# Eight samples of a head as one wide recurrence, and block sums moved to VectorE, in a one-core decoder layer

## Chip, cores, metric

One NeuronCore of a Trainium2 chip. The metric is the time of one execution on the device in microseconds, the median of several runs. "PE" is TensorE, "DVE" VectorE, "ACT" ScalarE, "POOL" GpSimd, "SP" SyncE, whose queue issues every transfer here.

## What is computed

One inference step of one layer with 512 prompt tokens and 8 single-token samples, 520 columns in all, width 2048, in float32. The part that the first half of the change touches is a gated recurrence of eight heads with a 128 x 128 state:

```python
f = lb + (1 - lb) * sigmoid(z_f);  k = 1 - f
S_t = diag(f_t) S_{t-1} + k_t (outer) i_t
o_t = S_t^T q_t                      # q after silu
```

The prompt starts from a zero state and is done by chunks of 128 tokens with matmuls. Each sample has a state of its own, is one token long, and gives an updated state (an output) and one vector o. The other parts: a gated unit with a layer norm, an output projection, and a dense feed-forward unit `(silu(h @ w_gate) * (h @ w_up)) @ w_down`.

## The kernel before, in words

Every matrix is held transposed, features on the 128 partitions and the 520 tokens along the columns, in two halves of 260. A float32 product is three matmuls of split operands (lines 103 to 105): a weight piece of 128 x 1024 is loaded into one of three raw buffers (`raw_piece`, line 70), ScalarE rounds it to its high part (line 82), VectorE subtracts for the low part (line 84). `pieces` keeps two pieces prepared ahead of the matmuls.

Python generators in the list `behind` are woven into the projections: each call of `step` advances every generator in it by one `yield`. The program order gives priorities; the scheduler of the framework then places an instruction in its engine's queue when its inputs are ready, earlier than in the program where it can. An engine's queue is run in order.

**The heads.** `head(h, w)` (line 321) is such a generator. Its steps, counted by its yields: 1 gates and logs; 2 cumulative sums and the decayed key kh, whose exponential is line 356 and whose last product is line 357; 3 silu of q and level 32; 4 the transpose of kh on PE (line 437) and level 8; 5 nothing; 6 and 7 scores of levels 32 and 8; 8 transpose of the input rows, and of the samples' packed decay, key and query, which go as 24 rows to a scratch tensor in DRAM (`scr`, line 465); 9 and 10 scores of levels 2 and 1; 11 the decays between chunks (matmuls of line 505, VectorE's line 509); 12 the output matmuls (lines 518 and 520); 13 squares; then the norm. Each head brings eight calls of `step`, two for each of its projections z, q, ib and g, so two heads overlap: step 9 of one is followed by step 1 of the next, its step 10 stands beside step 2 of the next, 11 beside 3, 12 beside 4.

**The samples.** The inner generator `samples` (line 469) does a head's eight samples in four pieces of two. A piece loads `bc` (line 475), in which the 24 rows are broadcast to all partitions (decay, key and query of two samples, 3 x 256 columns; one buffer), and two states `S` (line 477). Then VectorE multiplies the states by the decays (line 479), adds key times input, one instruction for each sample (line 483), the states are stored, and VectorE multiplies by the queries (line 486) and sums along the key (line 487). Piece 1 is loaded in step 8 and computed in step 9, where piece 2 is loaded, and so on to step 12.

**Feed-forward.** The first four blocks of columns are products as above. `combine` (line 656) runs beside half of them, and forms the differences of blocks of the activations for a scheme with seven instead of eight block products; of four differences for each of eight k, VectorE makes two (lines 660, 663) and GpSimd two (662, 665), and VectorE splits them (line 113). In the block stage after it, `quarters` (line 700) forms sums of weight blocks for each set of seven products: VectorE lines 717 and 719, GpSimd lines 720 and 725; the sums are split on lines 82 and 84 (their tile is named ws). The products are lines 736 to 738, in `term`.

Of the kernel before, what the change touches and what calls it, by code (L numbers as in the profile page):

```python
# [7 lines left out]
F32 = mybir.dt.float32  # L8
# [4 lines left out]
ALU = mybir.AluOpType  # L13
PSUM = bass.MemoryType.PSUM

P = 128
NP = 512
NS = 8
# [14 lines left out]
def trunk(ctx: ExitStack, tc: tile.TileContext, a: dict):  # L33
    nc = tc.nc
    vec, act, pe, sp = nc.vector, nc.scalar, nc.tensor, nc.sync
# [15 lines left out]
    def bank():  # L51
        return ax.tile([P, 512], F32, tag="ax", name="ax")

    def cols(h):
        return slice(h * HT, (h + 1) * HT)
# [5 lines left out]
    def full(pool, tag, bufs=1, dt=F32):  # L61
        return pool.tile([P, T], dt, tag=tag, name=tag, bufs=bufs)
# [17 lines left out]
    def halved(raw, n=1024):  # L80
        hi = wp.tile([P, 1024], F32R, tag="wh", name="wh", bufs=4)
        act.copy(hi[:, :n], raw[:, :n])  # L82
        lo = wp.tile([P, 1024], F32R, tag="wl", name="wl", bufs=4)
        vec.tensor_tensor(out=lo[:, :n], in0=raw[:, :n], in1=hi[:, :n].bitcast(F32), op=ALU.subtract)  # L84
        return hi, lo
# [22 lines left out]
    def split(x, pool, tag, bufs, scale=None):  # L108
        hi = part(pool, tag, bufs, F32R)
        lo = part(pool, tag, bufs, F32R)  # L110
        if scale is None:
            act.copy(hi, x)
            vec.tensor_tensor(out=lo, in0=x, in1=hi.bitcast(F32), op=ALU.subtract)
        else:
            act.mul(hi, x, scale)
            vec.scalar_tensor_tensor(out=lo, in0=x, scalar=scale, in1=hi.bitcast(F32), op0=ALU.mult, op1=ALU.subtract)
        return hi, lo
# [43 lines left out]
    for i in range(KT):  # L161
# [3 lines left out]
        if i % 4 == 0:  # L165
            c = slice((i % 8) * P, (i % 8 + 4) * P)
# [19 lines left out]
    for k in range(KT):  # L186
        X.append([split(x0[k][:, cols(h)], ap_, "A", 64, g1[:, k:k + 1]) for h in range(2)])
        for m in range(2):
            if k % 8 == 0:
                W[m].append([wp.tile([P, 1024], F32R, tag=t, name=t) for t in ("wh", "wl")])  # L190
            hi, lo = W[m][-1]
            raw = w0[m][k // 8]
            if k % 4 == 0:
                for o, n in ((0, 1), (1, 3)) if k == 0 else ((k % 8, 4),):
                    c = slice(o * P, (o + n) * P)
                    act.copy(hi[:, c], raw[:, c])
                    vec.tensor_tensor(out=lo[:, c], in0=raw[:, c], in1=hi[:, c].bitcast(F32), op=ALU.subtract)
            c = slice((k % 8) * P, (k % 8 + 1) * P)
# [48 lines left out]
    hp = ph1.enter_context(tc.tile_pool(name="hp", bufs=1))  # L247
# [73 lines left out]
    def head(h, w):  # L321
# [3 lines left out]
        k = full(hp, "k")  # L325
# [16 lines left out]
        b = hp.tile([P, NP], F32, tag="b", name="b")  # L342
# [63 lines left out]
        def scores(hh, kk, qq):  # L406
            for c2 in range(2):
                pl = bank()
                for c in range(2):
                    cg = 2 * c2 + c  # L410
                    pe.matmul(pl[:, c * 192:(c + 1) * 192], lhsT=kk[:, cg * P:(cg + 1) * P], rhs=qq[:, cg], start=True, stop=True)  # L411
                pv = pl[:, :384].rearrange("p (c t) -> p c t", c=2)
                Av = A[:, 2 * c2:2 * c2 + 2]
                off = 0
                for j in range(3):
                    n = (3 - j) * hh
                    if hh == 32:
                        act.copy(Av[32 * j:32 * j + 32, :, (j + 1) * 32:], pv[32 * j:32 * j + 32, :, off:off + n])
                        off += n
                    elif hh > 1:  # L420
                        g = 32 // hh
                        for c in range(2):
                            vec.copy_predicated(out=Av[:, c].rearrange("p (g t) -> p g t", g=g)[:, :, (j + 1) * hh:],
                                                mask=masks[hh][:, j * g:(j + 1) * g].unsqueeze(2).to_broadcast([P, g, n]),
                                                data=pv[:, c, off:off + g * n].rearrange("p (g t) -> p g t", t=n))
                        off += g * n
                    elif j < 2:
                        vec.copy_predicated(out=Av[:, j].rearrange("p (g t) -> p g t", t=2)[:, :, 1:2],
                                            mask=mone.unsqueeze(2), data=pv[:, j, 0:64].unsqueeze(2))
                        vec.copy_predicated(out=Av[:, j], mask=mdiag, data=pv[:, j, 64:192])  # L430
# [13 lines left out]
        ib = w["ib"]  # L444
# [19 lines left out]
        scr = tc.dram_tile([24, P], F32, name=f"scr{h}")  # L464
        sp.dma_start(scr, rows)
        ob = full(cc, "C", 16)
        O[8 + h] = ob

        def samples():

            n = 2
            for i in range(0, NS, n):
                bc = hp.tile([P, 3, n * P], F32, tag="bc", name="bc")
                rows_ = scr.rearrange("(a b) k -> a (b k)", a=3)[:, i * P:(i + n) * P]
                sp.dma_start(bc, rows_.partition_broadcast(P))
                S = hp.tile([P, n * P], F32, tag="S", name="S", bufs=2)
                sp.dma_start(S, a["state"][h][:, i * P:(i + n) * P])
                yield
                vec.tensor_tensor(out=S, in0=S, in1=bc[:, 0], op=ALU.mult)
                for b_ in range(n):  # L480
                    c = slice(b_ * P, (b_ + 1) * P)
                    t = NP + i + b_
                    vec.scalar_tensor_tensor(out=S[:, c], in0=bc[:, 1, c], scalar=ib[:, t:t + 1], in1=S[:, c],  # L483
                                             op0=ALU.mult, op1=ALU.add)
                sp.dma_start(a["o_ss"][h][:, i * P:(i + n) * P], S)
                vec.tensor_tensor(out=bc[:, 0], in0=S, in1=bc[:, 2], op=ALU.mult)
                vec.tensor_reduce(out=ob[:, NP + i:NP + i + n].unsqueeze(2), in_=bc[:, 0].rearrange("p (b k) -> p b k", b=n),
                                  op=ALU.add, axis=mybir.AxisListType.X)
            yield

        sg_ = samples()
        next(sg_)
        yield

        scores(2, *lv2)
        next(sg_)
        yield

        scores(1, *lv1)
        next(sg_)  # L500
        yield

        pd = bank()
        for c in range(4):
            pe.matmul(pd[:, c * P:(c + 1) * P], lhsT=kht[:, c], rhs=ibt[:, c], start=True, stop=True)
# [2 lines left out]
        for c in range(1, 4):  # L508
            vec.scalar_tensor_tensor(out=Sc[:, c], in0=Sc[:, c - 1], scalar=dec[:, c], in1=pd[:, c * P:(c + 1) * P],
                                     op0=ALU.mult, op1=ALU.add)  # L510
        sp.dma_start(a["o_sp"][h], Sc[:, 3])
        next(sg_)
        yield

        next(sg_)
        po = bank()
        for c in range(4):
            pe.matmul(po[:, c * P:(c + 1) * P], lhsT=ibt[:, c], rhs=A[:, c], start=True, stop=(c == 0))
            if c:
                pe.matmul(po[:, c * P:(c + 1) * P], lhsT=Sc[:, c - 1], rhs=qh[:, c * P:(c + 1) * P], start=False, stop=True)  # L520
        act.copy(ob[:, :NP], po)
        yield

        sq = full(hp, "e")
# [3 lines left out]
        for i in range(2):  # L528
# [3 lines left out]
                                     op0=ALU.mult, op1=ALU.mult)  # L532
# [123 lines left out]
    def combine():  # L656
        c0, c1 = cols(0), cols(1)
        for k in range(8):
            lo, hi = M[k], M[k + 8]
            vec.tensor_tensor(out=lo[:, c0], in0=lo[:, c1], in1=lo[:, c0], op=ALU.subtract)  # L660
            T1[k] = split(lo[:, c0], tp, "T", 48)
            nc.gpsimd.tensor_tensor(out=lo[:, c1], in0=hi[:, c1], in1=lo[:, c1], op=ALU.subtract)
            vec.tensor_tensor(out=hi[:, c1], in0=hi[:, c1], in1=lo[:, c0], op=ALU.subtract)
            T2[k] = split(hi[:, c1], tp, "T", 48)
            nc.gpsimd.tensor_tensor(out=hi[:, c0], in0=hi[:, c1], in1=hi[:, c0], op=ALU.subtract)
            T3[k] = split(lo[:, c1], tp, "T", 48)
            yield

# [31 lines left out]
    def quarters(w, i, first):  # L700

        raws = {}

        def load(q, src, pool, bufs):
            pool, bufs = (wp, 3) if first else (pool, bufs)
            raws[q] = pool.tile([P, 1024], F32, tag="wr", name="wr", bufs=bufs)
            sp.dma_start(raws[q], src)

        def m1():
            load("11", w[i, 0], wx, 4)  # L710
            load("21", w[i + 1, 0], wx, 4)
            load("22", w[i + 1, 1], wp, 3)
            return halved(raws["11"], 1024)

        def m6():
            s1 = raws["s1"] = wp.tile([P, 1024], F32, tag="wh", name="ws", bufs=4)
            vec.tensor_tensor(out=s1, in0=raws["21"], in1=raws["22"], op=ALU.add)  # L717
            s2 = raws["s2"] = wp.tile([P, 1024], F32, tag="wl", name="ws", bufs=4)
            vec.tensor_tensor(out=s2, in0=s1, in1=raws["11"], op=ALU.subtract)  # L719
            nc.gpsimd.tensor_tensor(out=raws["21"], in0=raws["11"], in1=raws["21"], op=ALU.subtract)  # L720
            load("12", w[i, 1], wp, 3)
            return halved(s2, 1024)

        def m5():
            nc.gpsimd.tensor_tensor(out=raws["s2"], in0=raws["12"], in1=raws["s2"], op=ALU.subtract)
            return halved(raws["s1"], 1024)

        return [m1, m6, m5, lambda: halved(raws["12"], 1024), lambda: halved(raws["21"], 1024),
                lambda: halved(raws["s2"], 1024), lambda: halved(raws["22"], 1024)]
# [13 lines left out]
    c0, c1 = cols(0), cols(1)  # L743
# [214 lines left out]
```

## Time and profile before

| | us |
|---|---|
| median of 3 runs | 2319.09 (2318.36 to 2325.36) |
| the profiled execution | 2318.88 |
| its span, first to last instruction | 2317.2 |
| PE busy | 2266.3 |
| DVE busy | 1664.3 |
| ACT busy | 1065.9 |
| POOL busy | 220.6 |

The span is one execution; a matmul's end is modelled, and busy time of PE is not its peak rate. "PEclk" in a window is the mean granted TensorE clock, 1.00 being 2.4 GHz and 0.50 being 1.2 GHz. The heads run from about 115 to 630 us, the output projection to about 890, the first feed-forward blocks with `combine` to about 975, the block stage to about 1790, the last product after that.

### The profile page before, as it was taken

The numbers are of one execution on the slowest core, as the hardware profiler recorded it, in microseconds if no ns is written. First come the engines' busy times: TensorE is split into PE (matmuls) and PEld (weight loads), VectorE is DVE, ScalarE is ACT, GpSimd is POOL, SyncE is SP. The second block draws the span as 40 slices with busy tenths as digits, with TensorE's granted clock in tenths as the row PEclk, the third lists the DMA queues.
The fourth block names the chain that finished last, engine by engine and source line by source line (L and its number), as shares of the span: only waits on it lengthen the run. The fifth ranks groups of instructions, "written<-read, shape, count | busy, mean of one in ns | idle before, by whom it ended". The sixth has DMA issues, their size and how long they took to land.

```text
span 2317.2 us, 44793 instructions
## 1 busy us (share of the span) xinstructions
PE 2266.3 (98%) x18548; PEld 2256.2 (97%) x18548; DVE 1664.3 (72%) x2688; ACT 1065.9 (46%) x1607; POOL 220.6 (10%) x116
## 2 busy tenths in 40 slices
PE   8999999999999998999999999999999999999998
PEld 8999999999999998999999999999999999999998
DVE  8398777777555778888888888888888534434367
ACT  7286566666345555444343443444334512212155
POOL 0000000000000000322222222222221000000000
PEclk9999999999999999999999999999999999999999
DMA  6224333443335766543333333333333723332275
GB/s 224 92 88 125 113 114 111 120 120 120 115 110 182 214 209 194 176 158 115 115 110 126 119 115 124 119 120 110 118 119 102 229 92 129 112 113 95 90 240 156
DMA packets 130267, 310.16 MB, mean 134 GB/s; under 512 B 14928, under 2 KB 57360, under 8 KB 130064
## 3 DMA queue, kind: packets, MB, share of 16 engines
q1 hardware_dynamic: 130064, 307.30, 42.7%
q8 instruction: 145, 2.38, 0.4%
q14 instruction: 58, 0.48, 0.1%
HBM read 281.64 MB, written 25.61 MB: 133 GB/s over the span
## 4 chain that ended last, share of the span: by engine, by line
PE 80%; DVE 9%; DMA 8%; ACT 1%; issue 1%; SPq 0%; DVEq 0%; POOL 0%; ACTq 0%; POOLq 0%
PE mm L105 14%; PE mm L104 14%; PE mm L103 14%; PE mm L738 8%; PE mm L736 8%; PE mm L737 8%; DMA bc<-scr 5%; PE ax L738 3%; PE ax L736 3%; PE ax L737 3%; DVE wl L84 2%; PE ax L411 1%; DMA scr<-rows 1%; DMA wr<-w_up 1%; DVE S L483 1%
## 5 line engine op out<-in xcount | busy, mean ns | idle before, releaser
L105 PE MATMUL mm<-A,wl 128*128 128x260 f32 x3616 | 1026.2, 284 | 8.7 <-DVE wl L84 8.4
L103 PE MATMUL mm<-A,wh 128*128 128x260 f32 x3616 | 1031.3, 285 | 2.0 <-ACT wh L82 2.0
L104 PE MATMUL mm<-A,wh 128*128 128x260 f32 x3616 | 1026.0, 284 | 0.0
L82 ACT CAST wh<-wr 128x1024 fp32r<-128x1024 f32 (+1 forms) x460 | 475.4, 1035 | 771.6 <-PE mm L104 475.4
L84 DVE TENSOR_TENSOR wl<-wr,wh 128x1024 fp32r<-128x1024 f32 (+1 forms) x460 | 554.7, 1207 | 268.4 <-ACT wh L82 255.8
L105 PEld LDWEIGHTS mm<-A,wl 128*128 128x128 f32 x3616 | 685.0, 189 | 10.5 <-DVE wl L84 10.3
L103 PEld LDWEIGHTS mm<-A,wh 128*128 128x128 f32 x3616 | 684.8, 189 | 2.5 <-ACT wh L82 2.2
L104 PEld LDWEIGHTS mm<-A,wh 128*128 128x128 f32 x3616 | 685.0, 189 | 0.3
L738 PE MATMUL mm<-A,wl 128*128 128x260 f32 x960 | 271.1, 282 | 0.5 <-DVE wl L84 0.5
L737 PE MATMUL mm<-A,wh 128*128 128x260 f32 x960 | 270.8, 282 | 0.0
L736 PE MATMUL mm<-A,wh 128*128 128x260 f32 x960 | 270.4, 282 | 0.0
L82 ACT CAST wh<-ws 128x1024 fp32r<-128x1024 f32 x120 | 123.8, 1047 | 265.8 <-DVE ws L719 265.8
L811 DVE TENSOR_TENSOR Y<-mm,Y 128x260 f32<-128x260 f32 x160 | 68.4, 427 | 193.0 <-PE mm L105 192.8
L84 DVE TENSOR_TENSOR wl<-ws,wh 128x1024 fp32r<-128x1024 f32 x120 | 188.4, 1570 | 11.8 <-ACT wh L82 10.8
L736 PE MATMUL mm<-T,wh 128*128 128x260 f32 x640 | 181.4, 283 | 1.3 <-ACT wh L82 1.3
L738 PE MATMUL mm<-T,wl 128*128 128x260 f32 x640 | 180.8, 282 | 0.8 <-DVE wl L84 0.8
L738 PEld LDWEIGHTS mm<-A,wl 128*128 128x128 f32 x960 | 180.2, 188 | 0.7 <-DVE wl L84 0.7
L737 PEld LDWEIGHTS mm<-A,wh 128*128 128x128 f32 x960 | 180.8, 188 | 0.0
L736 PEld LDWEIGHTS mm<-A,wh 128*128 128x128 f32 x960 | 180.7, 188 | 0.0
L737 PE MATMUL mm<-T,wh 128*128 128x260 f32 x640 | 180.1, 281 | 0.0
L720 POOL TENSOR_TENSOR wr<-wr 128x1024 f32<-128x1024 f32 x40 | 95.8, 2396 | 478.5 <-DVE ws L717 478.5
L719 DVE TENSOR_TENSOR ws<-ws,wr 128x1024 f32<-128x1024 f32 x40 | 134.3, 3358 | 0.0
(229 smaller groups left out, 3123.2 us busy)
## 6 DMA issues: line engine op xcount, KB each, us to landing
wr<-w_gate SPq DMA_DIRECT2D x96, 512.0 KB, 4.0
wr<-w_up SPq DMA_DIRECT2D x96, 512.0 KB, 4.1
wr<-w_down SPq DMA_DIRECT2D x96, 512.0 KB, 3.6
wr<-w_in SPq DMA_DIRECT2D x92, 512.0 KB, 4.1
wr<-w_out SPq DMA_DIRECT2D x64, 512.0 KB, 3.8
bc<-scr SPq DMA_DIRECT2D x32, 384.0 KB, 5.3
G<-fd SPq DMA_DIRECT2D x44, 260.0 KB, 3.9
fd<-G SPq DMA_DIRECT2D x40, 260.0 KB, 3.6
```

Of the source, the lines that this page charges most:

```text
L82: act.copy(hi[:, :n], raw[:, :n])
L84: vec.tensor_tensor(out=lo[:, :n], in0=raw[:, :n], in1=hi[:, :n].bitcast(F32), op=ALU.subtract)
L103: pe.matmul(ps[:, :HT], lhsT=wh[:, c], rhs=xh, start=(k == 0), stop=False)
L104: pe.matmul(ps[:, :HT], lhsT=wh[:, c], rhs=xl, start=False, stop=False)
L105: pe.matmul(ps[:, :HT], lhsT=wl[:, c], rhs=xh, start=False, stop=(k == n - 1))
L411: pe.matmul(pl[:, c * 192:(c + 1) * 192], lhsT=kk[:, cg * P:(cg + 1) * P], rhs=qq[:, cg], start=True, stop=True)
L719: vec.tensor_tensor(out=s2, in0=s1, in1=raws["11"], op=ALU.subtract)
L720: nc.gpsimd.tensor_tensor(out=raws["21"], in0=raws["11"], in1=raws["21"], op=ALU.subtract)
L736: pe.matmul(ps, lhsT=wh[:, c], rhs=xh, start=(start and k == 0), stop=False, skip_group_check=not start)
L737: pe.matmul(ps, lhsT=wh[:, c], rhs=xl, start=False, stop=False, skip_group_check=not start)
L738: pe.matmul(ps, lhsT=wl[:, c], rhs=xh, start=False, stop=(k == len(xs) - 1), skip_group_check=not start)
L811: vec.tensor_tensor(out=Y[m][:, cols(h)], in0=ps, in1=Y[m][:, cols(h)], op=ALU.add)
```

## The change

In `head`, the generator `samples` is gone. Step 8 issues one transfer of all 24 rows to `bc` (now 3 x 1024 columns) and one load of all eight states. Step 10 holds the scores of level 1 and the decays. Step 11 holds two products over 1024 columns, states by decays and keys by inputs; step 12 adds them after the output matmuls, stores the eight states in one transfer, multiplies by the queries and sums. In `combine` and `quarters`, four lines move from GpSimd to VectorE.

```diff
--- before.py
+++ after.py
@@ -466,40 +466,17 @@
         ob = full(cc, "C", 16)
         O[8 + h] = ob
 
-        def samples():
-
-            n = 2
-            for i in range(0, NS, n):
-                bc = hp.tile([P, 3, n * P], F32, tag="bc", name="bc")
-                rows_ = scr.rearrange("(a b) k -> a (b k)", a=3)[:, i * P:(i + n) * P]
-                sp.dma_start(bc, rows_.partition_broadcast(P))
-                S = hp.tile([P, n * P], F32, tag="S", name="S", bufs=2)
-                sp.dma_start(S, a["state"][h][:, i * P:(i + n) * P])
-                yield
-                vec.tensor_tensor(out=S, in0=S, in1=bc[:, 0], op=ALU.mult)
-                for b_ in range(n):
-                    c = slice(b_ * P, (b_ + 1) * P)
-                    t = NP + i + b_
-                    vec.scalar_tensor_tensor(out=S[:, c], in0=bc[:, 1, c], scalar=ib[:, t:t + 1], in1=S[:, c],
-                                             op0=ALU.mult, op1=ALU.add)
-                sp.dma_start(a["o_ss"][h][:, i * P:(i + n) * P], S)
-                vec.tensor_tensor(out=bc[:, 0], in0=S, in1=bc[:, 2], op=ALU.mult)
-                vec.tensor_reduce(out=ob[:, NP + i:NP + i + n].unsqueeze(2), in_=bc[:, 0].rearrange("p (b k) -> p b k", b=n),
-                                  op=ALU.add, axis=mybir.AxisListType.X)
-            yield
-
-        sg_ = samples()
-        next(sg_)
+
+        bc = hp.tile([P, 3, NS, P], F32, tag="bc", name="bc")
+        sp.dma_start(bc.rearrange("p a b k -> p a (b k)"), scr.rearrange("(a b) k -> a (b k)", a=3).partition_broadcast(P))
+        S = hp.tile([P, NS, P], F32, tag="S", name="S")
+        sp.dma_start(S.rearrange("p b k -> p (b k)"), a["state"][h])
         yield
 
         scores(2, *lv2)
-        next(sg_)
         yield
 
         scores(1, *lv1)
-        next(sg_)
-        yield
-
         pd = bank()
         for c in range(4):
             pe.matmul(pd[:, c * P:(c + 1) * P], lhsT=kht[:, c], rhs=ibt[:, c], start=True, stop=True)
@@ -509,16 +486,22 @@
             vec.scalar_tensor_tensor(out=Sc[:, c], in0=Sc[:, c - 1], scalar=dec[:, c], in1=pd[:, c * P:(c + 1) * P],
                                      op0=ALU.mult, op1=ALU.add)
         sp.dma_start(a["o_sp"][h], Sc[:, 3])
-        next(sg_)
-        yield
-
-        next(sg_)
+        yield
+
+        vec.tensor_tensor(out=S, in0=S, in1=bc[:, 0], op=ALU.mult)
+        vec.tensor_tensor(out=bc[:, 1], in0=bc[:, 1], in1=ib[:, NP:].unsqueeze(2).to_broadcast([P, NS, P]), op=ALU.mult)
+        yield
+
         po = bank()
         for c in range(4):
             pe.matmul(po[:, c * P:(c + 1) * P], lhsT=ibt[:, c], rhs=A[:, c], start=True, stop=(c == 0))
             if c:
                 pe.matmul(po[:, c * P:(c + 1) * P], lhsT=Sc[:, c - 1], rhs=qh[:, c * P:(c + 1) * P], start=False, stop=True)
         act.copy(ob[:, :NP], po)
+        vec.tensor_tensor(out=S, in0=S, in1=bc[:, 1], op=ALU.add)
+        sp.dma_start(a["o_ss"][h], S.rearrange("p b k -> p (b k)"))
+        vec.tensor_tensor(out=bc[:, 0], in0=S, in1=bc[:, 2], op=ALU.mult)
+        vec.tensor_reduce(out=ob[:, NP:].unsqueeze(2), in_=bc[:, 0], op=ALU.add, axis=mybir.AxisListType.X)
         yield
 
         sq = full(hp, "e")
@@ -659,10 +642,10 @@
             lo, hi = M[k], M[k + 8]
             vec.tensor_tensor(out=lo[:, c0], in0=lo[:, c1], in1=lo[:, c0], op=ALU.subtract)
             T1[k] = split(lo[:, c0], tp, "T", 48)
-            nc.gpsimd.tensor_tensor(out=lo[:, c1], in0=hi[:, c1], in1=lo[:, c1], op=ALU.subtract)
+            vec.tensor_tensor(out=lo[:, c1], in0=hi[:, c1], in1=lo[:, c1], op=ALU.subtract)
             vec.tensor_tensor(out=hi[:, c1], in0=hi[:, c1], in1=lo[:, c0], op=ALU.subtract)
             T2[k] = split(hi[:, c1], tp, "T", 48)
-            nc.gpsimd.tensor_tensor(out=hi[:, c0], in0=hi[:, c1], in1=hi[:, c0], op=ALU.subtract)
+            vec.tensor_tensor(out=hi[:, c0], in0=hi[:, c1], in1=hi[:, c0], op=ALU.subtract)
             T3[k] = split(lo[:, c1], tp, "T", 48)
             yield
 
@@ -717,12 +700,12 @@
             vec.tensor_tensor(out=s1, in0=raws["21"], in1=raws["22"], op=ALU.add)
             s2 = raws["s2"] = wp.tile([P, 1024], F32, tag="wl", name="ws", bufs=4)
             vec.tensor_tensor(out=s2, in0=s1, in1=raws["11"], op=ALU.subtract)
-            nc.gpsimd.tensor_tensor(out=raws["21"], in0=raws["11"], in1=raws["21"], op=ALU.subtract)
+            vec.tensor_tensor(out=raws["21"], in0=raws["11"], in1=raws["21"], op=ALU.subtract)
             load("12", w[i, 1], wp, 3)
             return halved(s2, 1024)
 
         def m5():
-            nc.gpsimd.tensor_tensor(out=raws["s2"], in0=raws["12"], in1=raws["s2"], op=ALU.subtract)
+            vec.tensor_tensor(out=raws["s2"], in0=raws["12"], in1=raws["s2"], op=ALU.subtract)
             return halved(raws["s1"], 1024)
 
         return [m1, m6, m5, lambda: halved(raws["12"], 1024), lambda: halved(raws["21"], 1024),
```

## Rows read from the trace of the kernel before

**Rows 1.** The page: its first line and part 1, busy time by engine.
```profile
span 2317.2 us, 44793 instructions
...
PE 2266.3 (98%) x18548; PEld 2256.2 (97%) x18548; DVE 1664.3 (72%) x2688; ACT 1065.9 (46%) x1607; POOL 220.6 (10%) x116
```

**Rows 2.** PE's waits: line, releaser: us in total, times, longest.
```profile
PE ax L437 <- DVE kh L357: 15.7, 8, 3.1
...
PE ax L520 <- DVE Sc L509: 5.1, 2, 2.9
...
PE mm L736 <- ACT wh L82: 1.3, 1, 1.3
```

**Rows 3.** Timeline of PE in one head: start, us, engine, line, operation.
```profile
500.67 0.63 PE L437 MATMUL ax<-ident,kh 128*128 128x128 f32 x4 [3.08 <-DVE kh L357]
```

**Rows 4.** Windows: us, busy time of each engine, PEclk, DMA share, GB/s.
```profile
187.00:196.00 9.00, 6.65 (x44) 6.46 (x43) 7.24 (x17) 5.27 (x9) 0.52 (x1) 0.81 0.38 91
...
314.00:326.00 12.00, 8.63 (x49) 8.18 (x48) 10.01 (x28) 4.84 (x8) 0.53 (x1) 0.72 0.42 148
...
437.00:447.00 10.00, 7.35 (x52) 7.19 (x51) 8.90 (x21) 5.50 (x8) 0.53 (x1) 0.83 0.44 141
```

**Rows 5.** VectorE's waits, the line of the samples' first instruction.
```profile
DVE S L479 <- DMA bc<-scr: 57.6, 26, 5.4
```

**Rows 6.** Timeline of VectorE and ScalarE between 486 and 501 us.
```profile
486.23 0.42 DVE L479 TENSOR_TENSOR S<-S,bc 128x256 f32<-128x256 f32 x1 [1.34 <-DMA bc<-scr]
...
486.96 0.69 DVE L335 SCALAR_TENSOR_TENSOR z<-z,sg 128x520 f32<-128x520 f32 x1
...
493.24 0.69 DVE L355 TENSOR_TENSOR kh<-b 128x512 f32<-128x512 f32 x1
...
495.79 0.63 ACT L356 ACTIVATE kh<-kh 128x512 f32<-128x512 f32 x1
...
497.09 0.42 DVE L479 TENSOR_TENSOR S<-S,bc 128x256 f32<-128x256 f32 x1 [2.90 <-DMA bc<-scr]
...
499.84 0.68 DVE L357 TENSOR_TENSOR kh<-kh,k 128x512 f32<-128x512 f32 x1
```

**Rows 7.** Timeline of SP's queue, the same head.
```profile
472.90 0.38 SPq L475 DMA_DIRECT2D bc<-scr  x1
```

**Rows 8.** Groups by line: busy us, mean ns | idle before, releasers.
```profile
L479 DVE TENSOR_TENSOR S<-S,bc 128x256 f32<-128x256 f32 x32 | 13.6, 425 | 62.9 <-DMA bc<-scr 57.6 <-issue 5.3
...
L483 DVE SCALAR_TENSOR_TENSOR S<-bc,ib,S 128x128 f32<-128x128 f32 x64 | 20.1, 345 | 0.2
...
L486 DVE TENSOR_TENSOR bc<-S,bc 128x256 f32<-128x256 f32 x32 | 13.3, 415 | 0.2
...
L487 DVE TENSOR_REDUCE C<-bc 128x2 f32<-128x256 f32 x32 | 13.1, 410 | 0.2
...
L717 DVE TENSOR_TENSOR ws<-wr 128x1024 f32<-128x1024 f32 x40 | 49.1, 1226 | 24.8 <-PE ax L737 21.9 <-DMA wr<-w_gate 2.9
```

**Rows 9.** DMA issues: count, KB each, median us to landing.
```profile
bc<-scr SPq DMA_DIRECT2D x32, 384.0 KB, 5.3
...
wr<-w_in SPq DMA_DIRECT2D x92, 512.0 KB, 4.1
```

**Rows 10.** Groups by line, block stage: VectorE beside GpSimd's sums.
```profile
L719 DVE TENSOR_TENSOR ws<-ws,wr 128x1024 f32<-128x1024 f32 x40 | 134.3, 3358 | 0.0
...
L84 DVE TENSOR_TENSOR wl<-ws,wh 128x1024 fp32r<-128x1024 f32 x120 | 188.4, 1570 | 11.8 <-ACT wh L82 10.8
```

**Rows 11.** Groups by line, `combine`.
```profile
L665 POOL TENSOR_TENSOR C<-C 128x260 f32<-128x260 f32 x8 | 12.2, 1527 | 7.5 <-DVE C L663 7.5
...
L113 DVE TENSOR_TENSOR T<-C,T 128x260 fp32r<-128x260 f32 x24 | 12.1, 526 | 0.0
```

**Rows 12.** Windows of `combine` and of the block stage.
```profile
931.00:971.00 40.00, 39.76 (x326) 39.34 (x326) 37.93 (x60) 22.27 (x42) 19.55 (x16) 1.00 0.63 188
...
1218.00:1276.00 58.00, 58.00 (x485) 58.00 (x484) 49.72 (x45) 21.48 (x27) 14.40 (x6) 1.00 0.37 118
```

## The prediction

> **What bounds the kernel now.** I read the page first. TensorE (PE) is busy 98% of a 2317.2 us span [rows 1], so only PE's idle time and stretches at the lower granted clock can be won. PE's waits come next [rows 2]: eight times the transpose of kh (line 437) waits for VectorE's product at line 357, 15.7 us in all; twice the output matmul of line 520 waits for the decays of line 509, 5.1 us. Both belong to the head stage, 20.8 us together. In the one shown [rows 3] PE stands 3.08 us until 500.67, so it was ready at 497.59.
>
> Each wait can cost twice. The stretches by window [rows 4] show a granted clock of 0.81, 0.72 and 0.83 around such waits, where it was full before PE stood still; the 0.83 row stands for three of 10 us (251:261, 437:447, 497:507). At half clock (1.2 instead of 2.4 GHz) half the work is done, so the loss is length times missing share: 9 x 0.19 + 12 x 0.28 + 3 x 10 x 0.17 = 1.7 + 3.4 + 5.1 = 10.2 us. The head stage thus holds 20.8 + 10.2 = 31.0 us; that is nearly all the change can reach there.
>
> Why is line 357 late? VectorE's waits [rows 5]: 26 times it stands at line 479 for the broadcast bc, 57.6 us. Its timeline in one head [rows 6] shows the place: two such waits, 1.34 and 2.90 us, lie in front of line 357, because the two-sample pieces of head 5 and the kh chain of head 6 share one in-order queue. bc has one buffer, so each piece's transfer is issued only after the reduction of the piece before.
>
> **The samples.** Removed per head: four pieces of one line 479, two of 483, one of 486, one of 487, or 4 x (0.425 + 2 x 0.345 + 0.415 + 0.410) = 7.8 us of VectorE durations [rows 8], and the four waits. Added: five instructions over 1024 columns. Line 717 has that width with two inputs, 1.226 us [rows 8]; the reduction scales as 0.410 + (1.226 - 0.425) = 1.21. Sum 6.1 us, so 1.7 us less busy per head; the waits matter more.
>
> Ahead of line 357 in rows 6 the change removes 1.34 + 2.90 of waits and two pieces less one reduction, 2 x 1.94 - 0.41 = 3.5, and puts two wide products there (step 11 runs beside step 3 of the next head), 2.45. Net 5.3 us, where 3.08 would do. The exponential before it [rows 6] ends at 495.79 + 0.63 = 496.42; even unmoved, line 357 could end at 497.10, before PE is ready. So I take the wait as gone in a head with a clear queue. What is late next: with a wide instruction just started, line 357 waits up to 1.23, on average half, 7 overlapping heads x 0.6 = 4.3. Head 0 has no samples before it; its 0.6 stays. I leave two heads their half clock, 2 x 1.7 = 3.4. Gain in the heads: 31.0 - 4.3 - 0.6 - 3.4 = 22.7 us. The best case is all 31.
>
> The decays (three of line 509 and four matmuls of line 505) move one step earlier, past one wait for bc; their cost is unchanged, and both waits of line 520 go (counted above).
>
> **The transfer.** On SP's queue twelve issues per head become three (one bc, one state, one store), 72 fewer in all, and the issues of bc behind reductions go, so weight loads are no longer held behind those. The one bc waits for scr as the first does now, and is issued at the same place, 472.90 [rows 7]. It moves 1536 KB at once, which the trace doesn't show. Ends: 5.3 us, as one piece of 384 KB lands now, to 4 x 5.3 = 21.2 [rows 9]. Its rows are 4 KB like those of a weight piece, 512 KB in 4.1, and three of those in series make 12.3; some of that is paid once, so I take 9, landing at 482. State and weights queue behind it; I cost that at nothing, since three raw weight buffers are loaded ahead and no wait of rows 2 lies in a head for want of weights. Without that cover a piece would be up to 9 us late.
> The first product sits in step 11, in program order about ten us after 482, but the scheduler may put it earlier in the queue, as it does with other ready work. Landing at 482 then still frees VectorE before line 335 is due at about 485.
> The Trainium skill, Perfetto Trace Analysis, DMA Optimizations, says that splitting transfers may let some start sooner, which speaks for the four pieces. Here the pieces can't start sooner, since one buffer chains them [rows 5 to 7]; by that rule the sum would have no gain in the heads, about 2318.
>
> **Sums of weight blocks.** In the block stage VectorE's line 719 takes 3.36 us beside GpSimd's sum, where line 717 of the same size takes 1.23 [rows 8, 10]; line 84 on such sums takes 1.57. After: 719 falls by 2.1, three of line 84 by up to 0.34 each against 1.23, and 2 x 1.23 come in: VectorE is lighter by about 0.7 us per set. PE has no idle there, 58.00 of 58 [rows 12], so the gain is nothing but at the first set, where PE waits 1.3 us for the cast behind 719 [rows 2]; I take 1, between 0 and 1.3. The cover is VectorE's 8 idle us of 58; should the new sums overrun it, the next cast would be late.
>
> In `combine` 16 sums move to VectorE, 16 x 0.42 = 6.7 us (line 479's size), where it is busy 37.93 of 40 us [rows 12]. Freed: lines 113 there take 0.526 [rows 11] against 0.42, so 24 x 0.10 = 2.5 at least; GpSimd's 1.53 us instances [rows 11] collide with others too, and lines waiting for their results stop waiting. Between -2.5 and +6.7 I take 0, since rows 10 show a hit instruction paying nearly all of GpSimd's time.
>
> **Sum.** The profiled execution took 2318.9 (span 2317.2 and 1.7 around it), 0.2 under the median. 2318.9 - 22.7 - 1 = 2295.2; with 0.2 added, **2295**. Its own range: 31.0 + 1.3 + 2.5 gained gives 2284; with twice the residue of the heads (8.3 more), 2304.
>
> **Rivals.**
> *Wide instructions take the place of the wait* (0.14). For: five of 1.2 us, none of which can be interrupted. If add, product and reduction all stand between the exponential's end and line 357, it starts at 496.42 + 3.66 = 500.08, against 499.84 now: nothing gained but line 520's 5.1 and the 1: **2313**. Against: they belong to step 12, behind line 357 in program order.
> The Trainium skill, Perfetto Trace Analysis, Optimizing Scalar/DVE Operations, says that where VectorE isn't saturated but causes bubbles, breaking up instructions may finish work sooner; that is this case, and rows 6 speak for it only in that the narrow pieces slip into gaps.
>
> *The one transfer lands late and the first product is early in the queue* (0.08). With both products in front of line 335, that starts at landing + 2.45 instead of 486.96, and 2.90 + 2.70 of waits and narrow work behind it are gone; break-even is a landing at 486.96 + 5.6 - 2.45 = 490.1, 17 us after issue. From there it is slower: at 21.2 us line 357 comes 4.0 later, 7 x 4.0 = 28, two more half-clock stretches 3.4, less 5.1 and 1: **2344**. Against: weight pieces of a third the size in 4.1 us.
>
> *The sums overload `combine`* (0.08): 6.7 us of wait and a half-clock stretch of 1.7 on top of the forecast, **2303**. For: VectorE at 95% there.
>
> **Chances.** Forecast 0.70. A measurement here tells 0.3%, 7 us, from no change: 2312 to 2326. Faster: 0.70 + 0.08 + 0.04 of the first rival (part of the way) = 0.82. Same: 0.10 of it and 0.02 of the second = 0.12. Slower 0.06. The range runs from 2284 to 2314, which takes in the first and third rival; left out are the late landing and anything better than all of the 31.
>
> **What would show it.** Right: no wait of VectorE for bc, or one per head; line 437's waits under 5 us in all, line 520's gone; granted clock full in the head stage; line 719 near 1.23; the block stage unchanged to the us. Wrong: line 437 still near 15 us with wide instructions directly in front of line 357 (first rival); a wait of several us at the first product (second); PE waiting for line 84 between 931 and 971 (third).

## The result, and the profile after

The changed kernel takes **2287.62 us** (2287.43 to 2288.51, four runs) against 2320.2 for the kernel before in the same comparison: ratio 0.9857, 95% interval 0.984 to 0.9874. The forecast was 2295, 2284 to 2314. Between the profiled executions the spans differ by 2317.2 - 2286.8 = 30.4 us.

The page of the changed kernel, first line and part 1, beside [rows 1]:

```profile
span 2286.8 us, 44310 instructions
...
PE 2256.1 (99%) x18548; PEld 2248.6 (98%) x18548; DVE 1583.0 (69%) x2664; ACT 1076.8 (47%) x1606; POOL 7.8 (0%) x20
```

PE is busy 10.2 us less with the same 18548 matmuls, which fits the 10.2 us that the forecast put down to half clock (between 191 and 194 us of the kernel before, at a clock of 0.50, PE starts 6 or 7 matmuls a us; at 1.00 beside it 10 or 11). PE's waits of the changed kernel, beside [rows 2]:

```profile
PE mm L105 <- DVE wl L84: 10.4, 5, 4.3
...
PE ax L437 <- DVE kh L357: 1.4, 4, 0.6
```

Line 437 waits 1.4 us where it waited 15.7. No row is left for the decays (5.1 us at line 520), nor for the cast behind which the block stage began (1.3 us). The first row is not of the heads: all of it lies between 662 and 960 us, and the kernel before had it too (8.4 us in 6). VectorE's wait for bc, 57.6 us in [rows 5], is now:

```profile
DVE S L491 <- DMA bc<-scr: 3.2, 5, 0.8
```

Windows of the changed kernel: from 115 us to the end of the head stage (the mark in the next paragraph), `combine` where it now runs (its sums stand at 905.1 to 939.1 us), the block stage (us, busy time by engine, PEclk, DMA share, GB/s):

```profile
115.00:661.90 546.90, 545.54 (x4439) 543.15 (x4438) 428.89 (x1006) 339.72 (x502) 5.60 (x13) 1.00 0.37 120
...
904.00:944.00 40.00, 40.00 (x328) 40.00 (x327) 38.36 (x77) 23.63 (x43) 0.00 (x0) 0.98 0.72 217
...
1010.00:1740.00 730.00, 730.00 (x6076) 730.00 (x6075) 560.03 (x635) 305.41 (x379) 0.00 (x0) 1.00 0.37 116
```

The head stage and the block stage in the kernel before:

```profile
115.00:691.20 576.20, 555.42 (x4433) 551.42 (x4432) 433.75 (x1125) 341.22 (x504) 6.33 (x13) 0.98 0.38 113
...
1010.00:1740.00 730.00, 730.00 (x6075) 730.00 (x6075) 626.35 (x561) 296.05 (x382) 172.80 (x72) 1.00 0.37 118
```

For the same work PE stands 546.90 - 545.54 = 1.4 us in the head stage where it stood 576.20 - 555.42 = 20.8, and is busy 9.9 us less, at full clock: 19.4 + 9.9 = 29.3. In the block stage PE was full from 1010 us on and stays full, though VectorE is 66 us less busy.

**Where the 30.4 us are.** Five marks cut the span: ScalarE's first scaling of a result of the output projection, its last, the first and the last product of the block stage, and the last output transfer. Before they stand at 691.2, 874.7, 982.1, 1789.9 and 2313.4; after at 661.9, 845.8, 955.1, 1759.5 and 2283.0. So the heads are 29.3 shorter, the output projection 0.4 longer (183.9 for 183.5), the first feed-forward blocks with `combine` 1.9 longer (109.3 for 107.4), the block stage 3.4 shorter (804.4 for 807.8), the rest equal (523.5). Sum -30.4.

**The same head as in [rows 6 and 7].** VectorE's queue after the change (start, us, engine, line, operation; in brackets how long the engine stood before it, and for what):

```profile
453.96 1.23 DVE L84 TENSOR_TENSOR wl<-wr,wh 128x1024 fp32r<-128x1024 f32 x1 [3.96 <-ACT wh L82]
...
460.43 1.23 DVE L491 TENSOR_TENSOR S<-S,bc 128x1024 f32<-128x1024 f32 x1 [0.80 <-DMA bc<-scr]
461.57 1.22 DVE L492 TENSOR_TENSOR bc<-bc,ib 128x1024 f32<-128x1024 f32 x1
462.83 1.23 DVE L501 TENSOR_TENSOR S<-S,bc 128x1024 f32<-128x1024 f32 x1
...
464.44 1.22 DVE L503 TENSOR_TENSOR bc<-S,bc 128x1024 f32<-128x1024 f32 x1
...
466.50 0.69 DVE L335 SCALAR_TENSOR_TENSOR z<-z,sg 128x520 f32<-128x520 f32 x1
...
472.11 1.21 DVE L504 TENSOR_REDUCE C<-bc 128x8 f32<-128x1024 f32 x1
...
474.97 0.68 DVE L355 TENSOR_TENSOR kh<-b 128x512 f32<-128x512 f32 x1
...
477.66 0.68 DVE L357 TENSOR_TENSOR kh<-kh,k 128x512 f32<-128x512 f32 x1
```

SP's queue and PE there:

```profile
453.53 0.33 SPq L471 DMA_DIRECT2D bc<-scr  x1
...
478.49 0.63 PE L437 MATMUL ax<-ident,kh 128*128 128x128 f32 x4 [0.28 <-DVE kh L357]
```

The order is not that of the program: four of the five wide instructions stand ahead of line 335, the reduction ahead of line 355. The data lies there 460.43 - 453.53 = 6.9 us after the issue. (This and the landings below are counted to the start of the first product.) One wait of 0.80 replaces 1.34 and 2.90.

The piece of line 84 with 3.96 us of waiting in front of it makes a common origin for this head in every kernel. In the kernel before it is

```profile
473.35 1.23 DVE L84 TENSOR_TENSOR wl<-wr,wh 128x1024 fp32r<-128x1024 f32 x1 [3.96 <-ACT wh L82]
```

Counted from there, PE was ready for the transpose at 500.67 - 3.08 - 473.35 = 24.24 us before, and at 478.49 - 0.28 - 453.96 = 24.25 after: the same. What moved is line 357, from 26.49 to 23.70.

Groups of the changed kernel, beside [rows 8, 10], and bc's transfer, beside [rows 9]:

```profile
L491 DVE TENSOR_TENSOR S<-S,bc 128x1024 f32<-128x1024 f32 x8 | 9.8, 1222 | 3.2 <-DMA bc<-scr 3.2
...
L504 DVE TENSOR_REDUCE C<-bc 128x8 f32<-128x1024 f32 x8 | 9.7, 1212 | 0.0
...
L702 DVE TENSOR_TENSOR ws<-ws,wr 128x1024 f32<-128x1024 f32 x40 | 48.7, 1217 | 0.0
...
L84 DVE TENSOR_TENSOR wl<-ws,wh 128x1024 fp32r<-128x1024 f32 x120 | 146.5, 1221 | 51.9 <-issue 50.5 <-PE mm L721 1.4
...
bc<-scr SPq DMA_DIRECT2D x8, 1536.0 KB, 6.5
```

Between 455 and 459 us the transfer of this head runs alone:

```profile
DMA packets 123, 1.51 MB, mean 378 GB/s; under 512 B 0, under 2 KB 0, under 8 KB 0
```

Its packets are of 1.51 MB / 123 = 12 KB, one for each partition, since the 24 rows lie one behind the other in `scr` and in the tile. The forecast had taken rows of 4 KB.

### The profile page after: what moved, and what is told of

Its sections match the earlier page's. It is cut to its first block, busy times and chain, and to the rows that moved or that the text cites. A ratio compares the mean times of both kernels' runs of the same rounds, so it can differ in the third digit from the quotient of the medians.

```text
span 2286.8 us, 44310 instructions
## 1 busy us (share of the span) xinstructions
PE 2256.1 (99%) x18548; PEld 2248.6 (98%) x18548; DVE 1583.0 (69%) x2664; ACT 1076.8 (47%) x1606; POOL 7.8 (0%) x20
## 4 chain that ended last, share of the span: by engine, by line
PE 91%; DVE 5%; DMA 2%; ACT 1%; issue 1%; SPq 0%; DVEq 0%; ACTq 0%
PE mm L105 17%; PE mm L103 17%; PE mm L104 17%; PE mm L719 8%; PE mm L721 8%; PE mm L720 8%; PE ax L721 3%; PE ax L719 3%; PE ax L720 3%; PE ax L411 2%; DMA bc<-scr 1%; DVE wl L84 1%; PE ax L128 0%; PE mm L202 0%; PE mm L203 0%
## 5 line engine op out<-in xcount | busy, mean ns | idle before, releaser
L105 PEld LDWEIGHTS mm<-A,wl 128*128 128x128 f32 x3616 | 682.4, 189 | 11.6 <-DVE wl L84 11.4
L84 DVE TENSOR_TENSOR wl<-ws,wh 128x1024 fp32r<-128x1024 f32 x120 | 146.5, 1221 | 51.9 <-issue 50.5
L720 PEld LDWEIGHTS mm<-T,wh 128*128 128x128 f32 x640 | 120.5, 188 | 0.0
L721 PEld LDWEIGHTS mm<-T,wl 128*128 128x128 f32 x640 | 120.4, 188 | 0.0
```

What stands on the lines that cost most here:

```text
L105: pe.matmul(ps[:, :HT], lhsT=wl[:, c], rhs=xh, start=False, stop=(k == n - 1))
L720: pe.matmul(ps, lhsT=wh[:, c], rhs=xl, start=False, stop=False, skip_group_check=not start)
L721: pe.matmul(ps, lhsT=wl[:, c], rhs=xh, start=False, stop=(k == len(xs) - 1), skip_group_check=not start)
```

## The experiments

The theory: pieces of bc chained by one buffer make VectorE stand in front of line 357; that wait is the loss, and the sums matter little. Rivals: the width of the instructions matters, or the decays' place, or GpSimd's collisions with VectorE. Ratios below are to the kernel before on the same chip in the same comparison, where it took 2321.9 to 2323.9.

### One part of the change at a time

**The samples without the sums.** The changed kernel with its four sums back on GpSimd:

```diff
-            vec.tensor_tensor(out=raws["21"], in0=raws["11"], in1=raws["21"], op=ALU.subtract)
+            nc.gpsimd.tensor_tensor(out=raws["21"], in0=raws["11"], in1=raws["21"], op=ALU.subtract)
...
```

> The changed kernel with the four block sums back on GpSimd, so the head part alone. Waiting theory (VectorE's waits for bc hold up line 357, PE waits and then runs at half clock): nearly the whole gain stays, 2287 to 2290 us, PE's waits for line 357 under 2 us in all. Rival (the sums on VectorE bring part of the gain): 2292 us or more.

2292.56, ratio 0.987 (0.9855 to 0.9885). Line 437 waits 1.0, and three waits at the start of the block stage are back (PE's waits):

```profile
PE mm L719 <- ACT wh L82: 1.5, 1, 1.5
PE mm L721 <- DVE wl L84: 1.2, 2, 0.8
```

Its block stage takes 808.0 us, as before. The bare median lies past the 2292 us that I had named for the rival, on a chip where the kernel before takes 2323.9; by the ratio nearly the whole gain stays. The rival is right in part: the sums bring some 3.4 us, all in the block stage. Part of the distance to the changed kernel is something else: a stretch at 782 to 790 us, in the output projection, has a granted clock of 0.57, worth 8 x 0.43 = 3.4 us at most; the projection takes 186.4 us instead of 183.9.

**The sums without the samples.** The kernel before with the same four lines on VectorE.

> The kernel before with the four block sums on VectorE and the heads as they were. Waiting theory: 2317 to 2320 us, line 357's waits still near 15 us, line 719 near 1.23 us, VectorE about 70 us less busy and nothing gained but some 1 us at the first set. Rival: 2314 us or less.

2319.4, ratio 0.998 (0.997 to 0.999). Line 437 waits 16.1 and line 520 4.5, as before; the block stage takes 804.5. Both runs agree: the sums shorten the block stage by 3.4, and the heads owe nothing to them.

**One transfer, narrow instructions.** The kernel before with one bc and one S for eight samples, and its two-sample instructions and the decays left where they were:

```diff
+            bc = hp.tile([P, 3, NS, P], F32, tag="bc", name="bc")
+            sp.dma_start(bc.rearrange("p a b k -> p a (b k)"), scr.rearrange("(a b) k -> a (b k)", a=3).partition_broadcast(P))
...
             for i in range(0, NS, n):
-                bc = hp.tile([P, 3, n * P], F32, tag="bc", name="bc")
-                rows_ = scr.rearrange("(a b) k -> a (b k)", a=3)[:, i * P:(i + n) * P]
-                sp.dma_start(bc, rows_.partition_broadcast(P))
...
```

> The kernel before with one transfer of bc and one of the states per head, but the narrow instructions of two samples, in their old steps, and the decays in their old step. Waiting theory: the waits go with the transfers, not with the width, so 2288 to 2294 us, PE's waits for line 357 under 4 us. Rival (fewer and wider instructions bring the gain): 2308 us or more, waits for line 357 above 10 us.

2292.53, ratio 0.9871 (0.9854 to 0.9887): what the samples alone gave. PE's wait and VectorE's:

```profile
PE ax L437 <- DVE kh L357: 0.6, 1, 0.6
```

```profile
DVE S L479 <- DMA bc<-scr: 3.2, 5, 0.8
```

The whole gain of the heads comes with the transfer (here the states' load is one as well; the run with two buffers below changes bc alone). Wide instructions add nothing that these runs can tell.

**The decays back in step 11.** The changed kernel with one `yield` moved up.

> The changed kernel with the decays back in step 11, after a yield of their own. Waiting theory: line 520's 5.1 us were a wait behind bc in the queue, not a late step, so 2287 to 2290 us and no wait for the decays above 1 us. Rival (moving the decays saved them): 2292 to 2294 us, PE waiting some 5 us for them.

2287.19, ratio 0.9846 (0.9831 to 0.986), line 437 at 0.6, no wait for the decays. Moving them was not needed: in the kernel before they were late because VectorE stood at bc. The narrow kernel above, with the decays in their old step, has no such wait either.

### Is it the chain or the width: the transfer in parts

**Two buffers for bc**, all else as before:

```diff
-                bc = hp.tile([P, 3, n * P], F32, tag="bc", name="bc")
+                bc = hp.tile([P, 3, n * P], F32, tag="bc", name="bc", bufs=2)
```

> The kernel before with two buffers for bc, nothing else. Waiting theory in its strong form (the single buffer chains the transfers): a piece is issued one piece earlier, so VectorE's waits for bc fall from 57.6 to under 25 us, line 357's waits from 15.7 to under 6, and half or more of the gain comes, 2290 to 2304 us at the time of before 2319. Rival (the transfers are late for another reason, the scratch store or the queue): 2312 us or more, line 357's waits above 10 us.

2307.25, ratio 0.9938 (0.9915 to 0.9961), slower than expected. VectorE's wait for bc is 17.6 us in 10 instances, PE's at line 437 7.7 in 6: loosening the chain by one link wins about half.

**The changed kernel with bc in four transfers** of two samples, all issued at once into the one tile:

```diff
-        sp.dma_start(bc.rearrange("p a b k -> p a (b k)"), scr.rearrange("(a b) k -> a (b k)", a=3).partition_broadcast(P))
+        for i in range(0, NS, 2):
+            sp.dma_start(bc[:, :, i:i + 2].rearrange("p a b k -> p a (b k)"),
+                         scr.rearrange("(a b) k -> a (b k)", a=3)[:, i * P:(i + 2) * P].partition_broadcast(P))
```

> The changed kernel with bc loaded by four transfers of two samples each into its parts, all issued in step 8. Waiting theory: what counts is that no transfer waits for a reduction, so within 2 us of the changed kernel, VectorE's wait at the first wide product under 20 us in all. Rival (one large transfer is what helps): 5 us or more slower than the changed kernel.

**2319.15, ratio 0.9983 (0.9968 to 0.9998).** I had expected the changed kernel's time. The gain is gone, although no transfer waits for another's buffer. VectorE in the same head:

```profile
472.47 1.23 DVE L84 TENSOR_TENSOR wl<-wr,wh 128x1024 fp32r<-128x1024 f32 x1 [3.96 <-ACT wh L82]
...
483.47 1.22 DVE L493 TENSOR_TENSOR S<-S,bc 128x1024 f32<-128x1024 f32 x1 [5.32 <-DMA bc<-scr]
...
489.54 0.69 DVE L335 SCALAR_TENSOR_TENSOR z<-z,sg 128x520 f32<-128x520 f32 x1
...
498.01 0.69 DVE L355 TENSOR_TENSOR kh<-b 128x512 f32<-128x512 f32 x1
...
500.70 0.68 DVE L357 TENSOR_TENSOR kh<-kh,k 128x512 f32<-128x512 f32 x1
```

Its transfers on SP's queue and the transpose on PE:

```profile
472.45 2.92 SPq L472 DMA_DIRECT2D bc<-scr  x4
...
501.53 1.09 PE L437 MATMUL ax<-ident,kh 128*128 128x128 f32 x4 [4.81 <-DVE kh L357]
```

All data is there 483.47 - 472.45 = 11.0 us after the first issue instead of 6.9. The wide product waits 5.32 instead of 0.80, 4.52 more, and PE waits 4.81 instead of 0.28, 4.53 more: from the product to PE nothing absorbs the delay. Over all heads line 437 waits 18.8 us in 6 instances, line 484 (the decays' matmuls) once 4.0 more, and the clock falls with them; from 501 to 511 us it is 0.83:

```profile
501.00:511.00 10.00, 9.47 (x68) 9.50 (x69) 8.65 (x20) 6.49 (x10) 0.00 (x0) 0.83 0.12 32
```

Two things could explain 11.0: more transfers, or shorter rows (pieces of 1 KB instead of 12). Two kernels vary them the other way round.

**Three transfers with rows of 4 KB** (decays, keys, queries):

```diff
...
+        for i in range(3):
+            sp.dma_start(bc[:, i].rearrange("p b k -> p (b k)"),
+                         scr.rearrange("(a b) k -> a (b k)", a=3)[i].partition_broadcast(P))
```

> The changed kernel with bc loaded by three transfers of 512 KB, each the decays, keys or queries of all eight samples, so rows of 4 KB as in the one transfer. If the short rows (1 KB) made the four transfers late: the last lands 6 to 8 us after the first issue, VectorE waits under 6 us at the first wide product, 2287 to 2293 us at a time before of 2319. If their number did: landing after 9 us or more, gain mostly gone, 2305 us or more.

2288.38, ratio 0.9856 (0.9839 to 0.9874): the gain is whole. The first product starts 459.20 - 453.61 = 5.6 us after the first issue, and no product waits for bc. It needs the first transfer only, which is in its favour; but the third, issued at 454.5, lands 6.2 us later, so all the data is there 7.1 us after the first issue, as with one transfer. (The expectation takes the one transfer's rows for 4 KB; its packets are of 12 KB, as shown above.)

**Two transfers of four samples**, rows of 2 KB, edited like the four.

> The changed kernel with bc loaded by two transfers of four samples, rows of 2 KB. If the rows' length counts: landing between that of the one (6.5 us) and of the four (11 us), some 7 to 9 us, and the time between the two, 2292 to 2310 us. If only the number of transfers counts: within 3 us of the changed kernel.

2300.5, ratio 0.9909 (0.9891 to 0.9927), between the two. In this head:

```profile
462.66 1.22 DVE L84 TENSOR_TENSOR wl<-wr,wh 128x1024 fp32r<-128x1024 f32 x1 [3.99 <-ACT wh L82]
...
471.20 1.23 DVE L493 TENSOR_TENSOR S<-S,bc 128x1024 f32<-128x1024 f32 x1 [2.88 <-DMA bc<-scr]
...
488.44 0.69 DVE L357 TENSOR_TENSOR kh<-kh,k 128x512 f32<-128x512 f32 x1
```

The issue is at 462.41, so the landing is 8.8 us after it, and PE waits 2.37:

```profile
489.27 0.63 PE L437 MATMUL ax<-ident,kh 128*128 128x128 f32 x4 [2.37 <-DVE kh L357]
```

Fewer transfers than three, and later: what orders the four kernels is the row length (12 and 4 KB level, then 2, then 1), not the count of transfers.

### Is it the place in the queue: the products pinned

**The four transfers again, with the two wide products kept where the program has them:**

```diff
-        vec.tensor_tensor(out=S, in0=S, in1=bc[:, 0], op=ALU.mult)
+        tc.keep_in_program_order(vec.tensor_tensor(out=S, in0=S, in1=bc[:, 0], op=ALU.mult))
...
```

> The wide kernel with four transfers, its two wide products kept at their place in the program (step 11) instead of being put early in VectorE's queue. Theory (a late landing costs only because the product stands early in an in-order queue): the wait for bc vanishes and the gain comes back though the transfers land no earlier, 2286 to 2292 us at a time before of 2319. Rival (the four transfers hurt in another way, by weights behind them or by the DMA engines): stays above 2308 us.

2290.98, ratio 0.9867 (0.9852 to 0.9883). The transfers are as slow as they were (up to 9.5 us from issue to landing, 9.4 without the pins), and the 28 us are back. VectorE in the same head:

```profile
457.13 1.23 DVE L84 TENSOR_TENSOR wl<-wr,wh 128x1024 fp32r<-128x1024 f32 x1 [3.96 <-ACT wh L82]
...
468.99 0.70 DVE L335 SCALAR_TENSOR_TENSOR z<-z,sg 128x520 f32<-128x520 f32 x1 [0.30 <-ACT k L328]
...
475.00 0.68 DVE L355 TENSOR_TENSOR kh<-b 128x512 f32<-128x512 f32 x1
475.60 1.22 DVE L493 TENSOR_TENSOR S<-S,bc 128x1024 f32<-128x1024 f32 x1
476.74 1.22 DVE L494 TENSOR_TENSOR bc<-bc,ib 128x1024 f32<-128x1024 f32 x1
...
479.09 0.69 DVE L357 TENSOR_TENSOR kh<-kh,k 128x512 f32<-128x512 f32 x1
```

Both products stand between lines 355 and 357, beside the exponential, and cost PE nothing here. So the late transfers hurt only through what was queued behind their consumer.

**One transfer, pinned too**, to see whether that beats the change:

> The changed kernel with the two wide products kept at their place in the program. Line 357's remaining waits (1.4 to 2.1 us) and VectorE's 3.2 us at bc go to nearly nothing; 0 to 3 us faster than the changed kernel, ratio to before 0.984 to 0.987. If the wide products then stand in front of line 357 and cost: waits of 1 us per head, 3 to 8 us slower.

2287.96, ratio 0.9852 (0.9836 to 0.9867): no difference from the changed kernel. With the data there after 6.9 us, the place doesn't matter.

One table, all counted from that head's line 84 (us; the rows are those above; the landings alone are counted from the issue):

| kernel | line 335 | line 357 | PE ready | PE waits |
|---|---|---|---|---|
| before | 13.61 | 26.49 | 24.24 | 3.08 |
| changed, landing 6.9 | 12.54 | 23.70 | 24.25 | 0.28 |
| two transfers, landing 8.8 | 14.61 | 25.78 | 24.24 | 2.37 |
| four transfers, landing 11.0 | 17.07 | 28.23 | 24.25 | 4.81 |
| four transfers, pinned | 11.86 | 21.96 | | |

### `combine`, and the changed kernel again

**`combine`'s two sums back on GpSimd**, the block sums left on VectorE.

> The changed kernel with the 16 sums of combine back on GpSimd, those of the weight blocks on VectorE. If combine's sums cost on VectorE what the sums-alone run suggests (first block product 1.5 us later), this is 1 to 3 us faster than the changed kernel; if contention with GpSimd costs as much, within 1 us.

2291.8, ratio 0.9875 (0.9859 to 0.9891). Beside it the changed kernel:

> The changed kernel itself, on the chip of the other runs of this call. Ratio to the kernel before within 0.984 to 0.988.

2289.25, ratio 0.9866 (0.9848 to 0.9884). The intervals overlap: moving `combine`'s sums neither helps nor hurts by an amount that this tells. In the one profile its block stage takes 805.5 us, 1.1 more than the changed kernel's, with one of the three waits (0.8) back.

No version here is measurably better than the changed kernel; the decays put back, three transfers and the pinned one stand level with it.

## Why the prediction was right, step by step

**What bounds the kernel: right.** The forecast put 31.0 us in the heads, 20.8 of waits and 10.2 of half clock. The waits at 437 fell by 14.3, the 5.1 at 520 went, and the head stage shows full clock: 14.3 + 5.1 + 10.2 = 29.6, against 29.3 by the marks.

**The heads' gain: mechanism right, size too small (22.7 for 29.3).** The residue was over-priced: 4.3 for seven heads in which line 357 would wait for a wide instruction, 0.6 for head 0, 3.4 for two stretches of half clock. The trace has 1.4 us of waits in all and no such stretch: 1.7 of the 31.0 is left, not 8.3. In the head shown no wide instruction catches line 357 at its start, because all five are through by then.

**Width and decays: right durations, no role.** Five instructions of 1212 to 1223 ns make the 6.1 us per head of the forecast. That the decays' waits would go was right; the reason was not the earlier step but the missing stalls (the run with the decays back).

**The transfer: inside its bounds, too slow by 2.** Taken at 9 us, it landed at 6.9, near the lower end of 5.3. The estimate went by rows of 4 KB and three weight pieces in series; the packets are of 12 KB, and no run shows 4 KB rows to be slower (three transfers: 7.1). Weights behind it were not late: no wait of PE shows it.

**Splitting.** Four transfers, chained by nothing, take 2319.15 where one takes 2287.62, and the times follow the row length: 12 and 4 KB level, then 2, then 1. The Trainium skill, Perfetto Trace Analysis, DMA Optimizations, says that smaller pieces may let some start sooner. Split along its long rows (three transfers) the first product does start sooner, 5.6 instead of 6.9 us after the issue, and the kernel gains nothing by it; split across them the runs speak against it, even without the chain for which the forecast set it aside. The same section's first rule, that small transfers carry overhead and are better batched, is put there for transfers under 2 KB; these are of 384 KB and more, so the runs agree with it only where it is read of the rows.

**The late-landing rival: right mechanism, wrong point.** It did not come, but its break-even of 17 us after issue was much too kind. Line by line, it read: line 335 starts 2.45 after the landing, and 5.60 behind it is saved. In fact line 335 starts 466.50 - 460.43 = 6.07 after the landing, since four wide instructions and small work stand there, not two: 3.62 later. And from line 335 to line 357 it is 11.16 us where it was 12.88, a saving of 1.72 and not 5.60, since the reduction and one more piece of line 84 moved in: 3.88 less. 17.2 - 3.6 - 3.9 = 9.7. The table gives the same: PE's 3.08 of before is reached at 6.9 + (3.08 - 0.28) = 9.7. Two transfers, at 8.8, keep 64% of the gain (0.0091 of 0.0143 by the ratios); four, at 11.0, keep 0.0017, about what the sums alone gave. So the forecast of 9 us, had it been true, would have been close to the edge: the 0.08 for this rival was too little, and the time was right partly because the transfer was quicker than I took it.

**The wide-instruction rival: its place came, its price did not.** The five do stand ahead of line 357, but before the exponential, in time that the stalls had taken. Where two stand beside the exponential (pinned), line 357 comes earlier still, at 21.96.

**The block stage: 3.4 instead of 1.** I counted PE's wait for the cast (1.3) and left out two just behind it for line 84, 1.2 us, all seen again above without the moved sums. In the kernel before:

```profile
986.43 0.39 PE L736 MATMUL mm<-T,wh 128*128 128x260 f32 x1 [1.29 <-ACT wh L82]
...
987.69 0.40 PE L738 MATMUL mm<-T,wl 128*128 128x260 f32 x1 [0.75 <-DVE wl L84]
...
994.21 0.39 PE L738 MATMUL mm<-A,wl 128*128 128x260 f32 x1 [0.50 <-DVE wl L84]
```

Waits are counted from the modelled end of the matmul before. By their starts, matmuls follow each other there every 0.12 us; these three start 1.57, 1.04 and 0.77 us after the one before, and the next after each only after 0.22 or 0.23. Together that is 3.3 us more than the usual pace, so the three waits are all but 0.1 of the 3.4. The bound of 1.3 was therefore wrong, and so was "the block stage unchanged to the us" among the signs of being right; that the other sets give nothing was right, since PE is full in both kernels.

**`combine`: 0, and level within the measurement.** Where `combine` now runs (904 to 944 us) VectorE is busy 38.36 of 40 us, 0.4 more than the 37.93 of before, and PE does not stand at all, so the third rival did not come. The stretch from the projection's end to the block stage is 1.9 us longer in the changed kernel; first before, then after:

```profile
874.70:982.10 107.40, 97.23 (x763) 95.46 (x763) 91.62 (x168) 59.27 (x106) 19.96 (x17) 0.95 0.64 190
```

```profile
845.80:955.10 109.30, 97.95 (x764) 96.51 (x763) 94.06 (x188) 60.99 (x109) 0.00 (x0) 0.95 0.64 187
```

PE stands 1.2 us longer (11.4 for 10.2) and is busy 0.7 longer; its waits are those of lines 103 and 105, ahead of `combine`. The kernel with one transfer and all sums on GpSimd shows 2.3 more than before, and over all the kernels here the stretch takes 106.5 to 110.1 us, wherever the sums stand, so it can't be put to the sums. Why these waits differ stays open.

**The sum.** -22.7 - 1 was forecast; -29.3 - 3.4 + 0.4 + 1.9 came. Of the 6.7 us between, the heads make 6.6 and the block stage 2.4, less 2.3 elsewhere.

## What to carry to other kernels

In an in-order queue, price a wait by what stands behind it, and measure both from a common origin in each kernel: here every microsecond of a late transfer came out at the matmuls. Here the scheduler put the consumer at the same early place in the queue however late its data came, so either bring the data early, in transfers with long rows, or pin the consumer behind the urgent work. Before calling a break-even far, list all the instructions that depend on the late data, not only the first.

## What was not expected of the hardware

- **Rows and speed.** While bc's packets run alone, the one transfer moves 378 GB/s at a DMA share of 0.95 (455 to 459 us, shown above). Packets of 2 KB (two transfers, 464 to 469 us) move 249 GB/s at a share of 0.76, packets of 1 KB (four transfers, 474 to 479 us) 226 at 0.89: engines that are nearly as busy move three fifths.

```profile
DMA packets 624, 1.25 MB, mean 249 GB/s; under 512 B 16, under 2 KB 16, under 8 KB 624
```

```profile
DMA packets 1146, 1.13 MB, mean 226 GB/s; under 512 B 41, under 2 KB 1146, under 8 KB 1146
```

- **GpSimd's neighbours.** With the sums gone from GpSimd, the second sum's line (719 before, 702 after) falls from 3358 to 1217 ns [rows 10], line 84 from 1570 to 1221, and an instruction over 520 columns that was not in the forecast, line 776 before and 759 after, from 2674 to 694 ns (block stage). The Trainium skill, Perfetto Trace Analysis, Optimizing Scalar/DVE Operations, says that the two engines share a read port, so that moving work between them might not help. The slower rows beside GpSimd fit a shared port; but moving the work did help VectorE, which takes 66 us less in the block stage with all the sums than without them. The kernel gains only the 3.4 us at its start by it, since PE was full.

- **Half clock comes and goes between like kernels.** In the heads of the pinned four-transfer kernel PE waits 1.9 us at line 437 and the clock stays at 1.00; the samples-alone kernel has a stretch of 0.57 in the output projection, where the change touches nothing. There PE waits 3.2 us at line 128; in the changed kernel it waits 2.6 and the clock stays at 1.00. Some microseconds between otherwise equal kernels are of this kind.
